# A two-layer diffusion backbone on one core: sums of squares in pieces with a product's step between, and roots spread by transposes

## The chip, the cores and the metric

The kernel runs on one core of a Trainium2 chip. The metric is the device time of one execution in microseconds; for a kernel it is the median of several runs. A profile is one execution taken by the hardware profiler. TensorE (PE, and PEld for its weight loads), VectorE (DVE), ScalarE (ACT), GpSimd (POOL) and SyncE (SP, which issues the transfers) run side by side and wait for each other through semaphores.

## The reference, cut to what matters

512 latent tokens and 256 context tokens of width 1024 pass two layers. Each layer norms its input with a modulation, projects it, runs three groups of heads (neighbourhood attention, differential attention, gated linear attention) on the projections, projects their outputs back onto the residual stream, norms again and runs a gated MLP with a convolution of width 3. Queries and keys of the first two groups are normed by head:

```python
def rms_norm(x, g):
    xf = x.astype(F32)
    y = xf * lax.rsqrt(jnp.mean(xf * xf, axis=-1, keepdims=True) + EPS)
    return (y * g.astype(F32)).astype(x.dtype)

xn = rms_norm(h, norm1[l]) * (1.0 + sc1) + sh1
qa = rms_norm(_heads(pl['qa'], NA_HEADS, HEAD_DIM), lp['qn_a'])
qb = rope_2d(rms_norm(_diff_heads(pl['qb']), lp['qn_b']), row, col)
o_b = rms_norm(o_b, lp['subln_b']) * (1.0 - lam_init)
```

The first line below the function is the modulated norm of the residual stream; the context tokens have their own. In the second layer the context tokens give keys, values and states only, and no outputs.

## The kernel before, in words

Activations lie with features on the partitions and tokens along the free axis, 128 features to a tile. Each fp32 product of the projections, the output projection and the MLP is made of three matmuls on rounded parts: high by high, high by low, low by high (`gemm_steps`, L251 to L253). A weight block of 512 KB is loaded (SP's queue), rounded by ScalarE (L262), and its remainder is taken by VectorE (L263), two blocks ahead.

In the mixer the order of TensorE's instructions is written out by hand. `weave` (L1121) takes a generator for the projections' products (`stream`, L606: the blocks named in `JOBS`, one after another; a step is three matmuls of 512 columns or six of 256, about every twelfth step is one of the modulation's own products, `ada_part`), and generators for the threads of the heads. The string `ORDER[layer]` says who comes next: a number is so many steps of the stream, a letter one step of a thread, lower case for the first two heads of a group and capitals for the second two. `next(stream, None)` does nothing once the stream is at its end. The letters that matter here:

- d: `da_prep` (differential attention: norms, rotation, stacks), a and b its two heads, e `da_out` (norms of its outputs);
- n: `na_prep` (neighbourhood attention: norms), l and r its two heads (for each tile of 128 queries: scores L897 to L899, softmax on VectorE and ScalarE, transposes in `to_tokens` L721, values L826);
- g: `gla_prep` (gated linear attention: gates L942 and L943, logarithms and running sums on ScalarE and VectorE), s its states, w its scores within chunks by levels (`gla_within`: L1018 to L1024 make a level's decays, two of the levels on POOL; L1049 is the product of the first two levels, L1061 that of the later ones), p and q its heads;
- h, f and o: the residual stream's return, the heads' outputs as operands, and the first part of the output projection, whose steps are products too.

`head_rms` (L673) is what the change touches in the threads d, e and n. It squares one or two tiles on ScalarE (L679), yields, and then sums the squares over a head's features: for each tile of 128 tokens one matmul whose weights are the 128 x 128 squares and whose moving operand is an indicator of 2 or 4 columns (L688). In layer 0 a call has 12 such products (d and n: 6 for the keys, 6 for the queries) or 6 (e); in layer 1, where queries have no context tokens, 10 or 4. An fp32 product is two records in the trace. The reciprocal roots come from `newton` (ten small operations of VectorE, L218 to L231) and are spread to the features by `head_bcast` (L706).

The modulated norm between the residual phases has its own sums (L489) and `newton`, and `norm_bcast` spreads the root of each token to all partitions by a matmul whose weights are the column of roots, broadcast, with the identity as moving operand (L494: two tiles of 128 tokens a call; `next_norm` calls it three times behind the output projection and three times behind the MLP in layer 0, and twice behind the output projection in layer 1). The very first norm does the same for six tiles in `begin` (L391).

PSUM tiles: `pg` (two buffers) for the stream's products, `pm` (two) for small ones, `pz` (two, of double size) for scores and broadcasts.

Of the kernel before, what the change touches and what calls it, by code (L numbers as in the profile page):

```python
# [27 lines left out]
EPS = 1e-6  # L28
NEG = -1e30
GW = 64  # L30
LEVELS = (64, 32, 16, 8, 4, 2, 1)
# row blocks of the output projection: those of the heads that are done first, and the last ones
OUT_A, OUT_B = (0, 1, 2, 3, 4, 5), (6, 7)
# dot products of the modulation's columns: along with a pair of blocks of the MLP, along with a block of its second product
CUTS = 2
ADA_F, ADA_D = 4, 2
# the order of the projections
JOBS = ("gates vb ka0 va0 qb1 kb1 kc0 vc0 qc0 qa1 ka1 va1 kc1 vc1 qc1 gc0 gc1 gc2 gc3",
        "qb0 kb0 vb qa0 ka0 va0 qb1 kb1 qa1 ka1 va1 gates kc0 vc0 qc0 gc0 gc1 kc1 vc1 qc1 gc2 gc3")
# the order of the first steps: norm, modulation by columns (scale, shift), rows of the products  # L40
# [13 lines left out]
# blocks of 32 columns whose windows of four say which copies a part of a stack goes to: (queries, keys) x (high, low)  # L54
# [3 lines left out]
# columns of the packed per-layer vectors  # L58
# [7 lines left out]
# column blocks of w_in (128 columns each)  # L66
# [4 lines left out]
class Lay:  # L71
    """Per-layer vectors on chip."""


class Rows:
    """Row blocks of a product's weights on two tiles of four."""
# [7 lines left out]
class Net:  # L84
# [53 lines left out]
    def setup(self, up):  # L138
        """Constants, and the first layer's vectors."""
# [14 lines left out]
    def tokens(self, p, up):  # L154
        """Two row blocks of the tokens."""
        x = up.tile([128, 2, TT], F32, name=f"x{p}")
        self.nc.sync.dma_start(out=x[:, :, :TL], in_=self.A["xT"][:, 2 * p:2 * p + 2])
        self.nc.sync.dma_start(out=x[:, :, TL:], in_=self.A["ctxT"][:, 2 * p:2 * p + 2])
        self.xs[2 * p], self.xs[2 * p + 1] = x[:, 0], x[:, 1]

    def silu_cond(self, up):
        """Twice silu of both conditioning vectors; the selector halves."""
# [28 lines left out]
    def layer_consts(self, y, up):  # L191
# [17 lines left out]
        # halved convolution weights (column 3 * f + j) and biases  # L209
# [4 lines left out]
    def newton(self, src, n, d):  # L214
        """rsqrt(src / d + EPS) of a compact [128, n]."""
# [8 lines left out]
        # a step of third order (to 8 / 3 of the root), and one of second order  # L224
# [21 lines left out]
    def gemm_steps(self, ps, w, ah, al):  # L246
        """A product; yields after every few steps of it."""
# [18 lines left out]
    def ada_part(self, y, part, pool, bufs):  # L266
        """A sixth of the modulation, 256 columns on each column tile; yields after every block of rows."""
# [22 lines left out]
    def ada_cols(self, fp, parts):  # L290
        """Sixths of the modulation [(layer, part)], columns on the partitions, by dot products of half columns; yields after each."""
# [24 lines left out]
    def ada_chunk(self, y, part, j, up):  # L316
        """256 columns of a sixth of the modulation: the blocks of rows on four column tiles."""
# [20 lines left out]
    def begin(self, y, up):  # L338
        """The first three products run on the scaled tokens; their outputs take the norm, and the shift's own product."""
# [42 lines left out]
        def norm():  # L382
# [5 lines left out]
            for (_, sl, _, _), p in zip(segs, (self.pg(TL), self.pm(TC))):  # L388
                t0 = sl.start // 128
                for t in range(t0, sl.stop // 128):  # L390
                    T.matmul(p[:, (t - t0) * 128:(t - t0 + 1) * 128], lhsT=r[:, t:t + 1].to_broadcast([128, 128]), rhs=self.ident,  # L391
                             start=True, stop=True)
                S.copy(bc[:, sl], p)
# [83 lines left out]
    def seg(self, g):  # L477
        """Stream, first token, operands of a segment."""
# [5 lines left out]
    def norm_bcast(self, accs):  # L484
        """PSUM [128, 256]: the reciprocal root mean square of each token on every partition."""
# [7 lines left out]
        for t in range(2):  # L493
            self.T.matmul(bc[:, t * 128:(t + 1) * 128], lhsT=r[:, t:t + 1].to_broadcast([128, 128]),  # L494
                          rhs=self.ident, start=True, stop=True)
        return bc

    def make_xn(self, y, xs, g, which, bc=None):
        """xs(k): the stream's tile and one for its norm (the same without bc: the tile is normed already)."""
# [30 lines left out]
    def pj(self, y, at, name, block, lat=True, ctx=True, perm=False, scale=1.0):  # L530
        """A block's product, on its way to DRAM, from where the head groups fetch it."""
# [17 lines left out]
    def cuts(self, y, name):  # L549
        """A weight that takes the place of two is made ready in parts."""  # L550
# [4 lines left out]
    def pjg(self, y, at, hd, ctxo):  # L555
        """A head's gate: twice its silu."""
# [14 lines left out]
    def pjv(self, y, at, name, block):  # L571
        """Values of 256 columns, tokens on the partitions."""
# [21 lines left out]
    def gates(self, y):  # L594
        """Low-rank gate activations: the weights' two parts side by side (the next product adds their sums)."""
# [35 lines left out]
    def finish(self, y, at, ctxo):  # L631
        """The heads' outputs as operands of the output projection."""
# [19 lines left out]
    def fetch(self, y, ea, hp, hd, cd):  # L652
        """The residual stream takes the place of the tiles that the heads needed first."""
# [10 lines left out]
    def out_first(self, y, ctxo):  # L664
        """The output projection of the heads that are done first."""
# [7 lines left out]
    def head_rms(self, at, xs, G, d, by=None):  # L673
        """Per (tile, token tile, group): reciprocal root mean squares (of the tile times by), compact. Yields ahead of the product."""
# [9 lines left out]
        for sq, (x, T) in zip(sqs, xs):  # L684
            offs.append(i)
            rhs = self.ones if G == 1 else self.ind[G]
            for t in range(T // 128):
                self.T.matmul(st[:, i * G:(i + 1) * G], lhsT=sq[:, t * 128:(t + 1) * 128], rhs=rhs, start=True, stop=True)  # L688
# [26 lines left out]
    def to_tokens(self, out, x, n):  # L715
        """x [128 features, n * 128 tokens] to out [128 tokens, n, 128 features]."""
# [15 lines left out]
    def da_prep(self, y, at, d, pr, ctxq):  # L732
# [8 lines left out]
        # the queries' norms go into the exponentials' scales  # L741
        qn = at.tile([128, TT], F32, tag="xn", name="xn", bufs=self.nxn)[:, :Tq]
        S.activation(qn, xq[:, :Tq], AF.Copy, scale=y.g[:, 1:2])
        for i, Tn in ((0, Tq), (1, TT)):
# [14 lines left out]
            # per component of 32 rows: high | low | high | low against high | low | low | high  # L759
# [22 lines left out]
        # reciprocals of the first softmaxes' sums  # L782
        d.rs = at.tile([128, 6, 2], F32, tag="rs", name="rs", bufs=2)

    def da_head(self, y, at, d, hh, ctxq):
        V, S, T = self.V, self.S, self.T
        for qt in range((TT if ctxq else TL) // 128):
# [18 lines left out]
            # times the first sum, whose reciprocal the outputs' norms take  # L806
# [13 lines left out]
    def values(self, d, qt, vs, ws):  # L820
        """Both heads' weights times values."""
# [7 lines left out]
    def da_out(self, y, at, d, pr, ctxq):  # L829
        """Norms of the outputs, and of the first softmaxes."""  # L830
# [34 lines left out]
    def na_head(self, y, at, d, pr, hh, ctxq):  # L865
# [3 lines left out]
        for qt in range(Tq // 128):  # L869
# [6 lines left out]
            # the scores' columns: segments (first, count, first key), and those with a bias  # L876
# [49 lines left out]
    def gla_prep(self, y, at, d, pr, ctxo):  # L926
        """Gates: 16 * log decay, then its running sums within chunks of 128, forward and backward."""
# [28 lines left out]
        # decays over whole chunks  # L956
# [5 lines left out]
    def gla_states(self, y, at, d):  # L962
        """States at the chunks' starts, both directions (context chunks are 4 and 5)."""
# [33 lines left out]
    def gla_within(self, y, at, d, ctxo):  # L997
        """Within chunks: pairs of halves at every level (whole blocks down to 32, then blocks of 32 side by side),
        then the diagonal (both directions: twice)."""
# [75 lines left out]
        # queries with the decay from their chunk's start, in the running sums' place  # L1075
# [5 lines left out]
    def gla_head(self, y, at, d, pr, hh, ctxo):  # L1081
        """Outputs, tokens on the partitions; root mean squares, then features on the partitions, and the gates."""
# [356 lines left out]
```

## Time and profile before

| | us |
|---|---|
| median of 3 runs | 1958.68 |
| lowest and highest run | 1957.72, 1968.63 |
| span of the profiled execution (first to last instruction) | 1956.1 |
| TensorE busy in it | 1874.8 |
| VectorE busy | 1234.8 |
| ScalarE busy | 774.1 |
| GpSimd busy | 107.1 |

Of the profiled execution the profile gives the span alone; it is 2.6 us below the median of the runs. The span holds two layers, one after the other: in layer 0 the mixer runs from about 60 to 560 us and the MLP to about 1130, in layer 1 the mixer from about 1160 to 1570 and the MLP to the end. In the rows, L12 is line 12 of the kernel; `pm<-k_ind,xn` reads "into tile pm from tiles k_ind and xn"; a bracket is the idle time ahead of an instruction and what ended it. PEclk is the clock granted to TensorE: 1.00 is 2.4 GHz, 0.50 is 1.2 GHz. A row of a stretch gives its bounds, its length, the busy time of PE, PEld, DVE, ACT and POOL (with the count of instructions; an engine without any is left out), then PEclk, the transfers' share and GB/s.

### The profile page before, as it was taken

To read this page: it belongs to the slowest core of one execution; us is meant where nothing else is said; L and a number is where in the kernel's file an instruction comes from. 1 tells how busy PE (TensorE), PEld (TensorE's weight loads), DVE (VectorE), ACT (ScalarE), POOL (GpSimd) and SP (SyncE) were. 2 spreads that over 40 slices of the span, in tenths; PEclk is the share of its full clock that TensorE was granted. 3 is DMA by queue.
4 is the path that set the end of the run, shared out by engine and by line. 5 is a ranking of instruction groups with operands and counts; after the bars stand their busy time and mean duration, and the time that the engine had idled before them with its cause. 6 is when DMAs were issued, how large, how long until landed. Compare 5 with 4: busy or idle time off the path is not lost. (4 is left out here: it accounts for less than half of the span.)

```text
span 1956.1 us, 33522 instructions
## 1 busy us (share of the span) xinstructions
PE 1874.8 (96%) x13598; PEld 1567.2 (80%) x13598; DVE 1234.8 (63%) x2554; ACT 774.1 (40%) x1350; POOL 107.1 (5%) x134
## 2 busy tenths in 40 slices
PE   8999999896999999999999999999996999999999
PEld 6778878774788888888888987878885788888887
DVE  6437575767669786588577563656576675445353
ACT  4536565455234331232133343645545343223232
POOL 2100000101020000000000110000012020000000
PEclk9989999897999999999999999999998989999999
DMA  9423242326122444234434223222433223332322
GB/s 323 138 92 111 92 146 98 115 98 204 54 74 92 124 129 149 94 125 130 139 109 127 95 68 130 84 81 68 143 106 101 65 72 97 97 97 86 109 94 100
DMA packets 90874, 217.93 MB, mean 111 GB/s; under 512 B 10464, under 2 KB 21472, under 8 KB 90592
## 3 DMA queue, kind: packets, MB, share of 16 engines
q1 hardware_dynamic: 90720, 215.79, 33.8%
q8 instruction: 107, 1.75, 0.4%
q14 instruction: 47, 0.39, 0.1%
HBM read 190.06 MB, written 25.69 MB: 110 GB/s over the span
## 5 line engine op out<-in xcount | busy, mean ns | idle before, releaser
L262 ACT CAST wh<-wr 128x1024 fp32r<-128x1024 f32 (+3 forms) x205 | 200.0, 978 | 415.9 <-PE pg L252 222.2
L263 DVE TENSOR_TENSOR wl<-wr,wh 128x1024 fp32r<-128x1024 f32 (+3 forms) x205 | 232.3, 1137 | 168.4 <-ACT wh L262 166.3
L252 PE MATMUL pz<-axl,wh 128*128 128x512 f32 (+1 forms) x752 | 288.3, 383 | 2.6 <-DVE axl L511 2.5
L251 PE MATMUL pz<-axh,wh 128*128 128x512 f32 (+1 forms) x752 | 287.8, 383 | 0.8 <-ACT axh L510 0.7
L253 PE MATMUL pz<-axh,wl 128*128 128x512 f32 (+1 forms) x752 | 287.0, 382 | 0.0
L252 PEld LDWEIGHTS pz<-axl,wh 128*128 128x128 f32 x752 | 142.3, 189 | 29.6 <-DVE axl L511 4.5
L251 PEld LDWEIGHTS pz<-axh,wh 128*128 128x128 f32 x752 | 142.3, 189 | 27.6 <-ACT axh L510 1.8
L253 PEld LDWEIGHTS pz<-axh,wl 128*128 128x128 f32 x752 | 142.3, 189 | 26.9
L308 DVE SCALAR_TENSOR_TENSOR wj<-wc,cb 128x512 bf16<-128x512 f32 x224 | 154.4, 689 | 6.2 <-DMA wc<-in_w_ada_t_dram 1.0
L251 PE MATMUL pg<-axh,wh 128*128 128x512 f32 x344 | 152.9, 445 | 2.7 <-ACT axh L262 2.5
L252 PE MATMUL pg<-axl,wh 128*128 128x512 f32 x344 | 139.3, 405 | 1.8 <-DVE axl L263 1.8
L253 PE MATMUL pg<-axh,wl 128*128 128x512 f32 x344 | 139.0, 404 | 0.0
L251 PE MATMUL pg<-gh,wh 128*128 128x512 f32 (+1 forms) x352 | 133.3, 380 | 0.0
L253 PE MATMUL pg<-gh,wl 128*128 128x512 f32 (+1 forms) x352 | 132.6, 377 | 0.0
L252 PE MATMUL pg<-gl,wh 128*128 128x512 f32 (+1 forms) x352 | 132.0, 375 | 0.0
L1161 DVE SCALAR_TENSOR_TENSOR h<-pg,ada,h 128x512 f32<-128x512 f32 (+1 forms) x80 | 53.5, 669 | 95.0 <-PE pg L253 94.8
L252 PE MATMUL pm<-acl,wh 128*128 128x256 f32 x352 | 99.8, 283 | 0.0
L253 PE MATMUL pm<-ach,wl 128*128 128x256 f32 x352 | 99.6, 283 | 0.0
L251 PE MATMUL pm<-ach,wh 128*128 128x256 f32 x352 | 99.5, 283 | 0.0
L801 DVE TENSOR_REDUCE sm<-pz 128x1 f32<-128x768 f32 (+1 forms) x80 | 67.4, 847 | 45.2 <-PE pz L800 44.5
L251 PEld LDWEIGHTS pg<-axh,wh 128*128 128x128 f32 x344 | 67.2, 195 | 30.8 <-issue 15.7
L1240 ACT ACTIVATE th<-cv 128x512 f32<-128x512 f32 x66 | 37.0, 561 | 121.2 <-DVE cv L1237 121.2
(387 smaller groups left out, 4194.9 us busy)
## 6 DMA issues: line engine op xcount, KB each, us to landing
wc<-in_w_ada_t_dram SPq DMA_DIRECT2D x112, 256.0 KB, 2.9
wr<-in_w_in_dram SPq DMA_DIRECT2D x45, 512.0 KB, 3.8
wr<-in_w_g_dram SPq DMA_DIRECT2D x44, 512.0 KB, 3.5
wr<-in_w_u_dram SPq DMA_DIRECT2D x44, 512.0 KB, 3.4
wr<-in_w_d_dram SPq DMA_DIRECT2D x31, 448.0 KB, 3.2
ar<-in_w_ada_dram SPq DMA_DIRECT2D x48, 256.0 KB, 3.3
ar<-in_w_ada_dram SPq DMA_DIRECT2D x16, 512.0 KB, 7.5
wr<-in_w_d_dram SPq DMA_DIRECT2D x16, 512.0 KB, 3.5
```

The source lines that it names most:

```text
L251: self.T.matmul(ps, lhsT=wh[:, k, :], rhs=ah[k], start=(k == 0), stop=False)
L252: self.T.matmul(ps, lhsT=wh[:, k, :], rhs=al[k], start=False, stop=False)
L253: self.T.matmul(ps, lhsT=wl[:, k, :], rhs=ah[k], start=False, stop=(k == n - 1))
L262: self.S.copy(hi, x)
L263: (eng or self.V).tensor_tensor(out=lo, in0=x, in1=hi.bitcast(F32), op=ALU.subtract)
L308: V.scalar_tensor_tensor(out=junk, in0=w, scalar=0.5, in1=cb[:, i, h * 512:h * 512 + 512], op0=ALU.mult, op1=ALU.mult, accum_out=acc[:, k, ...
L801: V.tensor_reduce(out=sm[:, c:c + 1], in_=s, op=ALU.max, axis=AX.X, negate=True)
L1161: self.late = V.scalar_tensor_tensor(out=h, in0=ps, scalar=y.ada[part][:, o, s:s + 1], in1=h, op0=ALU.mult, op1=ALU.add).ins
L1240: S.activation(th, c, AF.Tanh)
```

## The change

`head_rms` yields the mark `FILL` ahead of the third, fifth, seventh ... product of a call; `weave` answers each mark with one step of the projections' stream and then continues the same thread, before it reads on in the order string. The strings are unchanged. In `norm_bcast` and in the first norm the spreading matmuls become transposes of the broadcast column of roots (the same operands, one record instead of two). Comments and docstrings, which the diff also takes out, are left out here.

```diff
+FILL = "fill"
...
 def head_rms(self, at, xs, G, d, by=None):
...
             for t in range(T // 128):
+                if i and i % 2 == 0:
+                    yield FILL
                 self.T.matmul(st[:, i * G:(i + 1) * G], lhsT=sq[:, t * 128:(t + 1) * 128], rhs=rhs, start=True, stop=True)
                 i += 1
...
 def weave(self, stream, threads, order):
...
                 for _ in range(int(n or 0)):
                     next(stream, None)
-                if c:
-                    next(threads[c], None)
+                while c and next(threads[c], None) is FILL:
+                    next(stream, None)
...
 def norm(): (in begin)
-                    T.matmul(p[:, (t - t0) * 128:(t - t0 + 1) * 128], lhsT=r[:, t:t + 1].to_broadcast([128, 128]), rhs=self.ident,
-                             start=True, stop=True)
+                    T.transpose(p[:, (t - t0) * 128:(t - t0 + 1) * 128], r[:, t:t + 1].to_broadcast([128, 128]), self.ident)
...
 def norm_bcast(self, accs):
-            self.T.matmul(bc[:, t * 128:(t + 1) * 128], lhsT=r[:, t:t + 1].to_broadcast([128, 128]),
-                          rhs=self.ident, start=True, stop=True)
+            self.T.transpose(bc[:, t * 128:(t + 1) * 128], r[:, t:t + 1].to_broadcast([128, 128]), self.ident)
```

The ends of the two order strings, where the stream's last steps stand (the stream has 284 steps in layer 0 and 256 in layer 1; the numbers of a string add up to one more):

```
layer 0: ...wpqLR2RpqppRqqGLG2L1R1GSR1RL1L4p9R2RL1RqWL3R2RLR1fRWRffffffhhooSWSoSoSoWSWSooo...
layer 1: ...ws1s3w1w1wpq5ppqq4p2G1GqGSW15fffffffoWSooSWSoSooWooSoSWooo...
```

## Rows read from the trace of the kernel before

**Rows 1.** The page: TensorE's clock in 40 slices, and one group of transfers

```profile
PEclk9989999897999999999999999999998989999999
...
wr<-in_w_in_dram SPq DMA_DIRECT2D x45, 512.0 KB, 3.8
```

**Rows 2.** The sums of squares, line 688: all records of the run

```profile
L688 PE MATMUL pm<-k_ind,xn x216: 165/251/354, 87.7 to 1395.5; 128*128 128x2 f32 x64, 128*128 128x4 f32 x44
```

**Rows 3.** Timeline of TensorE, 118 to 141 us: start, duration, line, product, count

```profile
118.86 0.39 PE L253 MATMUL pg<-axh,wl 128*128 128x512 f32 x1
...
119.09 2.73 PE L688 MATMUL pm<-k_ind,xn 128*128 128x2 f32 x24
...
130.75 1.22 PE L770 MATMUL pm<-hl,stk 32*128 32x512 f32 x2
...
131.90 2.83 PE L706 MATMUL pz<-k_ident,ny 128*64 128x128 f32 x24
...
139.63 0.73 PE L770 MATMUL pm<-hl,stk 32*128 32x512 f32 x2
...
140.29 0.50 PE L251 MATMUL pg<-axh,wh 128*128 128x512 f32 x1
...
140.62 0.39 PE L252 MATMUL pg<-axl,wh 128*128 128x512 f32 x1
```

**Rows 4.** Stretches behind calls of the sums: length, engines' busy time, PEclk, DMA

```profile
91.70:95.10 3.40, 3.40 (x13) 1.36 (x12) 2.49 (x9) 1.16 (x2) 0.00 (x0) 0.50 0.32 91
...
122.40:139.40 17.00, 17.00 (x79) 10.87 (x78) 5.90 (x16) 1.79 (x3) 0.00 (x0) 0.50 0.21 69
...
177.10:180.40 3.30, 3.30 (x11) 2.16 (x10) 2.72 (x12) 0.86 (x2) 0.00 (x0) 0.50 0.15 40
...
263.00:266.40 3.40, 3.40 (x26) 3.23 (x27) 2.59 (x14) 2.53 (x4) 0.00 (x0) 1.00 0.00 0
...
358.00:364.70 6.70, 6.70 (x29) 5.61 (x33) 4.31 (x18) 1.34 (x4) 0.00 (x0) 0.50 0.01 4
...
378.50:385.20 6.70, 6.70 (x32) 6.17 (x32) 4.25 (x11) 2.74 (x3) 0.00 (x0) 0.50 0.08 22
...
1194.30:1197.60 3.30, 3.30 (x9) 2.20 (x8) 2.67 (x11) 0.62 (x1) 0.01 (x1) 0.50 0.69 231
...
1272.80:1279.50 6.70, 6.70 (x21) 5.50 (x22) 2.90 (x11) 0.95 (x3) 1.28 (x1) 0.50 0.45 137
```

**Rows 5.** Timeline of TensorE: four transposes, and four records of spreading products

```profile
427.48 0.66 PE L721 MATMUL pm<-k_ident,np 128*128 128x128 f32 x4
...
427.89 0.47 PE L251 MATMUL pg<-axh,wh 128*128 128x512 f32 x1
...
587.85 0.68 PE L494 MATMUL pm<-k_ident,ny 128*128 128x128 f32 x4 [0.85 <-DVE ny L231]
...
588.29 0.36 PE L253 MATMUL pz<-axh,wl 128*128 128x256 f32 x1
```

**Rows 6.** End of layer 0's stream: all engines, the stream's tiles alone, timeline

```profile
430.30:468.30 38.00, 29.73 (x208) 21.62 (x207) 30.08 (x63) 21.26 (x37) 4.79 (x4) 0.90 0.35 120
...
430.30:468.30 38.00, 19.65 (x117) 13.57 (x117) 4.03 (x10) 1.95 (x4) 0.90 0.35 120
...
459.16 1.76 DVE L1024 TENSOR_TENSOR lv<-lv,qk 128x1536 f32<-128x1536 f32 x1 [3.01 <-ACT lv L1023]
...
461.30 1.94 PE L276 MATMUL pg<-ar,csil 128*32 128x256 f32 x16 [4.60 <-DVE x L566]
...
468.27 1.99 PE L1049 MATMUL pz<-lv 64*64 64x64 f32 x64
```

**Rows 7.** End of layer 1's stream: the stream's tiles alone, timeline of TensorE

```profile
1481.00:1490.90 9.90, 9.82 (x42) 7.81 (x42) 0.66 (x1) 0.60 (x1) 1.00 0.18 65
...
1502.28 1.13 PE L1049 MATMUL pz<-lv 64*64 64x64 f32 x32 [11.38 <-DVE lv L1024]
...
1506.75 1.13 PE L1049 MATMUL pz<-lv 64*64 64x64 f32 x32 [3.34 <-DVE lv L1024]
```

More of the change, by code (lines that the diff above doesn't have):

```diff
@@ L71 @@
 class Lay:
+    pass
 class Rows:
```

## The prediction

> **What bounds the kernel now.** I read the page first, then the rows of the line that the change splits, then the stretches behind it, then the two places where the order of TensorE's work runs dry. The page shows TensorE busy for 1874.8 of 1956.1 us (the table above), and a granted clock below full in several slices [rows 1]. So TensorE's own order is the path nearly everywhere, and time is won by a higher clock or lost by a wait on it. The time to start from is this one profile's span, 1956.1 us; the median of the runs shown, 1958.68 us, is 2.6 us above it, and I add changes to the median.
>
> The sums of squares are 216 records, two for each of 108 products (12 calls of the helper) [rows 2]. A call of 24 records at 119.09 us takes 2.73 us, 0.11 us a record, with two columns each: the array has almost nothing to stream [rows 3]. What follows is the point. Behind seven of the twelve calls the clock goes to 0.50, the 1.2 GHz level. One step of the differential attention's stacks took 1.15 us there (130.75 to 131.90), and 0.66 us at the 2.4 GHz level (139.63 to 140.29): 43% of a slow stretch is lost [rows 3]. The slow stretches behind the calls last 3.4, 17.0, 3.3, 6.7, 6.7, 3.3 and 6.7 us, and each begins during its call or a few us behind it; behind the other five the clock stays at 1.00, as from 263.0 us behind a call of 12 records [rows 4].
>
> **The change part by part.**
>
> *Where the steps go.* A FILL comes ahead of the third, fifth, ... product of a call, and each one takes one step of the projections' stream. In layer 0 calls have 12, 12 and 6 products, so 5 + 5 + 2 FILLs for a pair of heads and 24 for the layer; in layer 1 they have 10, 10 and 4, so 4 + 4 + 1, and 18. The order strings are not changed. Counting their numbers, the stream (284 steps in layer 0, 256 in layer 1) ended with one call to spare; now it ends 24 and 18 steps sooner, and the numbers near the end of the strings find nothing. No work is added: steps move from the end of the mixer to the middle.
>
> *The clock, a gain.* Between two pieces of four records (4 x 0.11 = 0.44 us) there are now three products of 512 columns, about 0.7 us (118.86 to 119.09 is one: 0.23 us) [rows 3]. TensorE then streams for more than half of the time, where it did for hardly any. I take the six stretches in which a call of 20 or 24 records alone precedes the fall as gone: 3.4 + 17.0 + 3.3 + 6.7 + 3.3 + 6.7 = 40.4 us; at 43% that is 17.4 us [rows 3, 4]. The one at 378.5 us lies behind a call of only 12 records that follows other small products; I count half of 6.7 x 0.43 = 2.9, so 1.5. Gain 18.9 us; the bounds are 0 (the pieces don't hold the clock) and 20.3 us (all seven go).
>
> *The seams, a loss.* A large product that follows small ones starts late: its successor comes 0.33 us after it (140.29 to 140.62) rather than 0.23 [rows 3]. 42 more seams at 0.09 us cost 3.8 us. Below it is 0, if the next weights are loaded ahead; above it is twice as much, 7.6 us, at the low clock. I take 3.8, the value at the clock that I expect.
>
> *The transposes, a small gain.* The spreading product is two records and the trace's transposes are one. Four spreading records take 587.85 to 588.29, 0.44 us, and four transposes 427.48 to 427.89, 0.41 us for twice as many tiles [rows 5]. So each of the eight calls for a modulated norm (three in each of two places of layer 0, two in layer 1) gets about 0.22 us shorter, 1.8 us, and the first norm's six tiles save 0.6. Where TensorE waits for the norm this is on the path, and where it does not it is TensorE's time; 2.0 us, between 0 and 2.6.
> Here the Trainium skill speaks against the change: "TensorE: Matmul & The Clock Gate", Part 4 (PE-mode transpose), says that a transpose does not count as TensorE being busy as a matmul does, so that the full clock does not engage for it. By that rule the eight calls would come nearer to a fall of the clock; that is the last rival. The transposes of the trace stand among larger products [rows 5], so no row here settles it.
>
> *Dry end of layer 0, a loss.* The second gate product of the second pair of heads ends at 430.3 us, and the first scores within chunks of this pair (L1049) start at 468.27. In these 38.0 us the tiles of the stream hold TensorE for 19.65 us, the last of them at the low clock; all but one of the 24 missing steps fell here, and at the full clock they are 19.65 - 0.43 x 1.94 (the modulation's products at 461.30) = 18.8 us [rows 6]. This work now stands ahead of that stretch, where TensorE is full, and delays its start by 18.8. In return the stretch can shrink, but not below its own chain: gates, logarithm, running sums, decays of two levels on VectorE, ScalarE and POOL. This had its last product of decays at 459.16 + 1.76 = 460.9 us, 30.6 us after the gates, with VectorE busy for 30.08 of the 38.0, of which 4.03 us belonged to the stream's tiles and leave too [rows 6]. Between 27 (the chain less those) and 38 us (nothing shrinks) I take 29, nearest to the chain that the trace shows. Loss 18.8 - 9 = 9.8 us, bounds 7.8 and 18.8. The wait of 4.60 us of the modulation's product for VectorE at 461.30 goes [rows 6], but what is late next is this chain.
>
> *Dry end of layer 1, a loss.* Here TensorE already waits: the stream ends at 1490.9 and L1049 follows at 1502.28 after 11.38 idle us, its second half at 1506.75 after 3.34 more [rows 7]. Fourteen steps, 9.82 us, lie between the gates and that wait, and 4 more ahead of the gates: 18 steps of 3 x 0.23 us, 12.4 us, are done sooner and push everything behind [rows 3, 7]. Of the 4 ahead of the gates (2.8 us) I let half come back, 1.4, an estimate: the transposes between the two gate products then wait for VectorE. VectorE's running sums are freed of two operations of 0.66 us on the stream's last tiles, 1.3 us [rows 7]. Loss 12.4 - 1.4 - 1.3 = 9.7 us; bounds 8.3 (all 2.8 and the 1.3 come back) and 12.4.
>
> *What else the moved steps issue.* Their weights' loads (SP's queue; 3.8 us for a block that feeds 8 or 12 steps [rows 1]), ScalarE's rounding, VectorE's remainder and the copy out move with them. Each step's work keeps its order in each queue, and the blocks are about 8 us of TensorE apart, so I count nothing; if a FILL met a block not yet ready, sums and the square root behind them would wait for it. The sums' PSUM tile is held for about 3.5 us longer, while no other thread's product can come between. Nothing else is queued behind it on TensorE.
>
> Sum: -17.4 - 1.5 - 2.0 + 3.8 + 9.8 + 9.7 = +2.4 us. Forecast: no change that can be measured, 1958.7 + 2.4 = 1961.1 us; its own range is 1953 to 1969.
>
> **The rivals.**
>
> 1. *The dry ends shrink with the work.* If threads ran ahead as the stream does, the 19.5 us would be nothing: 1941.6 us. For it: 8.3 of the 38 us were idle on TensorE in layer 0, and its order, not the chain, held L1049 for the last 7 us. Against it: VectorE alone has 26 us of other work there, and in layer 1 it is TensorE that waits [rows 6, 7].
> 2. *The dry ends are paid in full (the other side).* Without steps between, the neighbourhood attention's rounds (scores, softmax, transposes, values) stand bare, at the low clock, and L1049 stays 38 us behind the gates. Then 18.8 + 12.4 = 31.2 instead of 19.5: 1972.8 us. The other terms make -17.1, so the kernel is slower from the point where the two stretches give back less than 14.1 of the 31.2; I count 11.7, and here it is 0. For it: 11.38 us of waiting at 1502.28 already; against it: the 4.60 us wait that goes.
> 3. *The clock falls all the same,* since each piece is still four small products and the steps between are single ones: the 18.9 us stay lost, 1980.0 us. For it: the slow stretch at 378.5 us, behind a call of only 12 records; against it: the steps at 139.63 us mix small and large products as thinly at the high clock [rows 3].
> 4. *Transposes let the clock fall at the norms.* Four more stretches of 3.4 us at 43% are 5.8 us: 1966.9 us. No row prices a transpose so, and eight short calls are little; its chance is small.
>
> **How the numbers follow.** Forecast 0.43, rival 1 0.15, rival 2 0.22, rival 3 0.10, rival 4 0.06, none of these 0.04. Within 1% is 1939.1 to 1978.3 us, about what a measurement of this kernel can tell from no change: forecast, rivals 2 and 4 and most of rival 1 lie inside. Faster by more needs rival 1 with the upper clock gain and no seams: 0.07. Slower by more is half of rival 3 and the upper ends of rival 2 and of the unnamed: 0.10. Same 0.83. The range leaves out rival 3 and about half of rival 1: 1942 to 1974 us.
>
> **What would show it.** Right: groups of four records of L688's line with three products of the stream between them; the clock at 1.00 behind the calls of 20 and 24; the stream's last product ahead of or near the second pair's gates in both layers; TensorE idle for about 20 us between the gates and L1049 in layer 1 (14.7 before); one record for each spread root. Wrong: the clock at 0.50 within 4 us of the split calls (rival 3), L1049 less than 24 or more than 34 us behind the gates in layer 0 (rivals 1, 2), new slow stretches at the norms (rival 4).

## The result, and the profile after

The changed kernel takes 1986.88 us (median of 4 runs, 1984.97 to 1987.51) against 1958.2 of before (the three runs of the table and one more, of 1951.24): a ratio of 1.0154, 95% interval 1.0113 to 1.0195. Here and below the ratio is an estimate from all runs and is not quite the quotient of the medians. The forecast of no change (1961.1 us) was wrong, and the time lies above its range. The profiled execution has a span of 1984.4 us, 28.4 more than that of before.

The page of the changed kernel: the span, the busy time of the engines, and the granted clock in 40 slices.

```profile
span 1984.4 us, 33478 instructions
...
PE 1870.5 (94%) x13576; PEld 1561.9 (79%) x13576; DVE 1233.7 (62%) x2554; ACT 775.9 (39%) x1350; POOL 110.7 (6%) x134
...
PEclk9999999985899999999999999999997989999999
```

TensorE is busy for 4.3 us less than before, and the kernel is 28 us longer: what was added is waiting. And the low clock has moved: the dips in slices 3 and 8 of [rows 1] are gone, and those in slices 10 (446 to 496 us) and 31 (1488 to 1538 us), where the two orders run out of steps, are deeper, with 5 instead of 7 and 7 instead of 8.

One split call, in the timeline of TensorE (start, duration, line, product, count):

```profile
121.38 0.50 PE L690 MATMUL pm<-k_ind,xn 128*128 128x2 f32 x4
121.74 0.48 PE L253 MATMUL pg<-axh,wh 128*128 128x512 f32 x1
122.05 0.40 PE L254 MATMUL pg<-axl,wh 128*128 128x512 f32 x1
122.29 0.40 PE L255 MATMUL pg<-axh,wl 128*128 128x512 f32 x1
122.52 0.50 PE L690 MATMUL pm<-k_ind,xn 128*128 128x2 f32 x4
122.88 0.48 PE L253 MATMUL pg<-axh,wh 128*128 128x512 f32 x1
```

The change does what it says (L690 is L688 of before). A piece of four records lets the next product start 0.36 us after it (121.38 to 121.74), 0.09 us a record instead of 0.11; the step behind it takes 0.78 us (121.74 to 122.52) instead of 3 x 0.23. The seam costs the 0.09 us that was forecast, and the piece gives as much back.

The stretches behind the calls, as [rows 4] (length, busy time of PE, PEld, DVE, ACT and POOL, PEclk, DMA), and the two ends:

```profile
127.00:144.00 17.00, 17.00 (x120) 11.94 (x119) 10.90 (x23) 6.63 (x11) 0.00 (x0) 1.00 0.24 86
...
366.00:372.80 6.80, 6.80 (x73) 5.16 (x76) 4.79 (x18) 1.88 (x4) 0.00 (x0) 1.00 0.39 130
...
1296.40:1303.20 6.80, 6.80 (x46) 6.06 (x45) 4.13 (x14) 2.63 (x5) 1.29 (x1) 1.00 0.43 128
436.80:484.60 47.80, 30.62 (x211) 20.87 (x208) 31.11 (x66) 23.23 (x40) 4.94 (x5) 0.50 0.20 69
1508.60:1539.30 30.70, 10.13 (x86) 7.07 (x87) 19.45 (x32) 14.89 (x17) 7.64 (x4) 0.50 0.09 31
```

Behind the calls the clock is now at 1.00, in those 17 us too that were at 0.50 before. At the end of layer 0's stream it is at 0.50 for 47.8 us on end, with TensorE idle for 17.2 of them.

To see where the 28 us came from I cut each mixer at two marks: G1, the first gate product of the second pair of heads (L942, in the changed kernel L944), and N, the norm's sums behind the mixer (L489, L490). Before: first call to G1, G1 to N, for layer 0 and then layer 1 (which I count from the norm's sums behind layer 0's MLP):

```profile
87.70:423.00 335.30, 326.73 (x2984) 260.47 (x2982) 202.50 (x470) 168.02 (x341) 12.30 (x19) 0.94 0.34 113
423.00:564.30 141.30, 120.69 (x1353) 95.26 (x1352) 97.20 (x199) 59.53 (x102) 13.79 (x16) 0.93 0.35 112
...
1131.10:1477.50 346.40, 334.58 (x2791) 276.67 (x2791) 212.54 (x493) 170.71 (x331) 16.94 (x28) 0.98 0.29 97
1477.50:1574.30 96.80, 77.74 (x819) 61.20 (x818) 68.25 (x129) 43.55 (x66) 17.16 (x14) 0.91 0.30 91
```

The same four in the changed kernel:

```profile
88.00:430.00 342.00, 330.41 (x3090) 264.63 (x3088) 207.63 (x481) 173.62 (x350) 13.24 (x19) 0.99 0.35 118
430.00:582.50 152.50, 117.82 (x1248) 91.65 (x1247) 91.89 (x188) 55.37 (x92) 13.78 (x16) 0.79 0.26 89
...
1147.40:1502.60 355.20, 339.21 (x2827) 280.02 (x2827) 212.79 (x487) 175.15 (x337) 20.35 (x28) 1.00 0.30 100
1502.60:1602.40 99.80, 70.18 (x777) 54.53 (x775) 67.68 (x133) 40.07 (x60) 16.20 (x14) 0.85 0.22 72
```

In layer 0, 106 records of TensorE have gone from behind G1 to ahead of it: 42 of 512 columns, 48 of 256 and 16 of the modulation, some 16 us at the full clock (0.23 and 0.12 us between successive starts; the modulation's counted at 0.04). The stretch up to G1 is only 6.7 us longer, and G1 comes 7.0 us later: the higher clock made TensorE's busy time some 12 us less than the old one and the 16 (330.4 for 326.7 + 16), but its waits are 3.0 us longer (11.6 for 8.6, length less busy time), so about 9 came back. But the stretch behind G1, relieved of that work, has become 11.2 us longer, at a clock of 0.79 instead of 0.93. In layer 1, 42 records (9.7 us) went the same way; G1 is 8.8 us later against the layer's start, although the busy time is some 5 us less than the sum, since the waits are 4.2 us longer (16.0 for 11.8); the stretch behind it is 3.0 us longer. With -1.9 between N of layer 0 and layer 1's start (566.8 us before, 564.9 after) the sum is 7.0 + 11.2 - 1.9 + 8.8 + 3.0 = 28.1 of the 28.4 us. These are differences of two single profiles; the experiments show how far such parts scatter.

The end of layer 0's stream in the timeline, as [rows 6] (a bracket is the idle time ahead and what ended it):

```profile
435.06 0.62 PE L278 MATMUL pg<-ar,csil 128*32 128x256 f32 x4 [1.67 <-DVE nt L231]
436.64 0.97 PE L278 MATMUL pg<-ar,csil 128*32 128x256 f32 x4 [0.95 <-DMA ar<-in_w_ada_dram]
...
442.03 1.06 PE L945 MATMUL pz<-asb,wa 64*128 64x256 f32 x2
...
459.42 1.09 PE L723 MATMUL pm<-k_ident,np 128*128 128x128 f32 x4 [8.34 <-DVE np L912]
...
473.47 1.12 PE L828 MATMUL pm<-wn,vn 128*64 128x128 f32 x6 [2.32 <-ACT wn L724]
...
478.49 0.66 PE L723 MATMUL pm<-k_ident,np 128*128 128x128 f32 x2 [1.79 <-DVE np L912]
479.08 2.84 PE L1051 MATMUL pz<-lv 64*64 64x64 f32 x96
```

The second gate product ends at 443.1 us and L1051 starts at 479.08: 36.0 us, where the forecast took 29 and before had 38.0. So the 11.2 us come from the two sides of this stretch: from G1 to the end of the second gate product 13.1 us instead of 7.3 (the waits for the modulation in the first two rows, and the low clock), and from L1051 to N 103.4 instead of 96.0.

The chain behind the gates did not get shorter: its last product of decays is the last of the next rows, and ends 31.4 us after the gates (30.6 before). The first row is of before, the others are of the changed kernel; L949 and L951 begin VectorE's part of the chain.

```profile
435.97 1.76 DVE L949 TENSOR_TENSOR lt<-B,lt 128x1536 f32<-128x1536 f32 x1 [0.59 <-ACT lt L948]
...
447.13 1.58 ACT L950 ACTIVATE lt<-lt,ones 128x1536 f32<-128x1536 f32 x1
...
451.11 0.48 DVE L1117 SCALAR_TENSOR_TENSOR xn<-pm,gq,xn 128x256 f32<-128x256 f32 x1 [0.78 <-PE pm L1115]
451.51 1.75 DVE L951 TENSOR_TENSOR lt<-B,lt 128x1536 f32<-128x1536 f32 x1
...
472.73 1.76 DVE L1026 TENSOR_TENSOR lv<-lv,qk 128x1536 f32<-128x1536 f32 x1 [3.01 <-ACT lv L1025]
```

In the 36 us VectorE is busy for 23.4, so it is not its load that sets this chain. From L951 to the last of VectorE's decays (L1024, done at 463.07) it takes 11.6 us instead of 14.6, so the work that left did free it. But in before L949 starts as soon as the logarithm of ScalarE is done; here the logarithm is done at 448.71 and L951 starts 2.8 us later, behind operations of VectorE's queue that wait for TensorE's products at the low clock (L1117). Another 1.1 us go at the two hand-overs to ScalarE and POOL behind it. And TensorE, left with the neighbourhood attention's small products, waits for each softmax in turn (8.34, 2.32 and 1.79 us of the rows); the last such round stands between the end of the chain at 474.5 us and L1051.

The end of layer 1's stream, as [rows 7]:

```profile
1508.51 1.05 PE L1115 MATMUL pm<-k_ident,ox 128*128 128x128 f32 x4 [4.31 <-DVE ox L1106]
...
1511.36 1.06 PE L945 MATMUL pz<-asb,wa 64*128 64x256 f32 x2
1530.83 1.14 PE L1051 MATMUL pz<-lv 64*64 64x64 f32 x32 [18.41 <-DVE lv L1026]
1534.12 1.14 PE L1051 MATMUL pz<-lv 64*64 64x64 f32 x32 [2.16 <-DVE lv L1026]
```

Here TensorE idles for 20.6 us ahead of L1051, as forecast (about 20; 14.7 before), and 4.31 more ahead of the second gate product.

### The profile page after: what moved, and what is told of

It is laid out like the page before. It is cut to its first block, busy times and chain, and to the rows that moved or that the text cites. A ratio compares the mean times of both kernels' runs of the same rounds, so it can differ in the third digit from the quotient of the medians.

```text
span 1984.4 us, 33478 instructions
## 1 busy us (share of the span) xinstructions
PE 1870.5 (94%) x13576; PEld 1561.9 (79%) x13576; DVE 1233.7 (62%) x2554; ACT 775.9 (39%) x1350; POOL 110.7 (6%) x134
## 5 line engine op out<-in xcount | busy, mean ns | idle before, releaser
L807 ACT ACTIVATE P<-pz,sm,ny 128x768 f32<-128x768 f32 (+1 forms) x80 | 72.6, 908 | 32.3 <-DVE sm L806 29.3
```

Of the source, the lines that this page charges most:

```text
L807: S.activation(P[:, c, :nk], s, AF.Exp, bias=sm[:, c:c + 1], scale=rq, accum_out=sm[:, 2 + c:3 + c])
```

## The experiments

The ratios are against runs of the kernel before on the same chip, with 95% intervals. The theory held at first was that moving the steps out of the ends costs the time and the clock behind the calls is a gain; the rivals are in the expectations.

**The steps paid back from the next numbers.** Each mark's step is taken off the numbers that follow, none below 1, so that the streams end where they did.

```diff
+        owed = 0
...
-                for _ in range(int(n or 0)):
+                n = int(n or 0)
+                back = min(owed, max(n - 1, 0))
+                owed -= back
+                for _ in range(n - back):
                     next(stream, None)
                 while c and next(threads[c], None) is FILL:
+                    owed += 1
                     next(stream, None)
```

> The kernel after, but each step of the stream that a mark takes is paid back from the next numbers of the order string (never below one step a number), so the stream reaches its end at the same letter as before the change. Theory A (the clock gain is real and the dry ends ate it): both dry ends are as before, no slow stretch behind the split calls, 1958 - 14 to 19 = 1939 to 1944 us. Rival B (splitting the sums costs more than the clock gives: seams, later roots): at or above 1958 us.

1978.51 us, ratio 1.0103 (1.0071 to 1.0136): the expected gain is missing. The ends are as before in layer 0 (141.3 us from G1 to N; 100.7 in layer 1, where four profiles with the order of before have 96.8 to 101.6). But where steps were taken, TensorE waits, and the clock falls behind it, as in this place of layer 1 (a wait for the operands of the differential attention's stacks, then the stretch behind it):

```profile
1198.81 0.50 PE L772 MATMUL pm<-hl,stk 32*128 32x512 f32 x1 [1.90 <-ACT hl L264]
...
1199.70:1213.40 13.70, 13.70 (x69) 7.75 (x70) 1.78 (x3) 1.70 (x3) 0.00 (x0) 0.50 0.22 71
```

Layer 0 comes out as in before (N at 563.1 us), layer 1 20.8 us longer up to N. About half of that is TensorE's waiting, 41.0 us instead of 30.9, and half the clock, at 0.50 for 54.6 us instead of 30.7. The way of paying back cost what the ends had saved.

**The calls whole, the steps behind each.**

```diff
+                marks = 0
                 while c and next(threads[c], None) is FILL:
+                    marks += 1
+                for _ in range(marks):
                     next(stream, None)
```

> The kernel after with the calls whole again: all the steps that a call's marks take run behind its last product. The dry ends stay as in the kernel after, the splitting goes. Theory A: the slow stretches behind the calls come back in part, about 14 us more than the kernel after, 1995 to 2003 us. Rival B (the splitting is the cost): back to about 1960 us.

1989.86 us, 1.0174 (1.013 to 1.0217): neither. Against the changed kernel the difference is some 3 us and the intervals overlap, so that the cut itself is not shown to be worth anything. Up to G1 of layer 0 the two profiles say why:

```profile
87.40:428.40 341.00, 334.68 (x3089) 267.73 (x3087) 208.49 (x481) 173.51 (x350) 13.24 (x19) 0.97 0.35 118
```

The changed kernel took 342.0 us for the same records. Its cuts kept the clock higher (at 0.50 for 6.8 us, here for 17.0), but it waited for 11.6 us and this kernel for 6.3. The changed kernel's longest wait there, for the roots of a cut call that ends later, does not occur here; its row in the changed kernel:

```profile
278.86 2.00 PE L708 MATMUL pz<-k_ident,ny 128*64 128x128 f32 x24 [4.14 <-DVE ny L699]
```

So the pieces do hold the clock, which here still falls behind six of the twelve calls of the two layers, for 3.4 or 6.8 us each, and behind none in the changed kernel. But steps right behind a whole call already shorten the slow stretches (3.4 us from 125.4, where before had 17), and what cutting adds to the clock it takes back in waits. The loss at the ends is nearly the same (148.5 and 100.5 us from G1 to N).

**The transposes alone,** in the kernel before (the two edits at L391 and L494).

> The kernel before with the transposes alone. Theory A: 1 to 3 us less than before, 1955 to 1957 us, and no new slow stretch at the norms. Rival D (transposes let the clock fall at the norms): up to 6 us more, 1964 us.

1954.4 us, 0.9992 (0.9968 to 1.0015): no difference that can be measured. Its windows: first call to G1, G1 to N, and the norms behind layer 0's mixer and MLP.

```profile
86.90:416.60 329.70, 322.02 (x2983) 256.25 (x2981) 202.34 (x470) 167.77 (x341) 12.30 (x19) 0.96 0.34 115
416.60:557.10 140.50, 120.76 (x1354) 95.27 (x1353) 97.11 (x199) 59.43 (x102) 13.81 (x16) 0.93 0.34 113
...
557.10:590.00 32.90, 29.95 (x227) 27.58 (x227) 28.99 (x85) 16.08 (x36) 9.24 (x12) 1.00 0.10 33
1122.00:1152.00 30.00, 27.95 (x191) 24.46 (x192) 24.08 (x76) 12.99 (x27) 3.20 (x4) 1.00 0.18 63
```

The clock is at 1.00 over both norms, and the time leaves no room for the last rival's 6 us (the upper end of the interval is 3). Behind layer 1's mixer, where the other two calls are, the clock is at 0.50 for 10.2 us with transposes as in before. That is also the answer of this case to the Trainium skill's "TensorE: Matmul & The Clock Gate", Part 4 (PE-mode transpose), by which the full clock does not engage for a transpose: eight calls of two, among other products, did no harm that can be measured.

The first row says something else. Up to G1 this is the order of before, and it took 329.7 us instead of 335.3, with the clock at 0.50 for 27.3 us instead of 37.5. One profile of an unchanged order differs from another by 6 us there, so the 9 us that came back in layer 0 against the profile of before are under 4 against this one. A third profile of this order, of the kernel below with cuts in layer 1 alone, sides with it:

```profile
87.60:416.80 329.20, 321.94 (x2983) 256.11 (x2981) 202.07 (x470) 167.71 (x341) 12.29 (x19) 0.96 0.34 115
```

**The clock kept up at the ends.** Where a number finds the stream ended, a product that nobody reads is computed. It adds work and takes away no wait.

```diff
+    def idle_product(self):
+        self.T.matmul(self.pg(384), lhsT=self.ident, rhs=self.cosT[:, :384], start=True, stop=True)
...
-                    next(stream, None)
+                    if next(stream, self) is self:
+                        self.idle_product()
```

> The kernel after, and wherever a number of the string finds the stream at its end, a product of 384 columns of constants that nobody reads (0.64 us at the high clock; 44 of them, so 28 us of useless work). Theory C (the dry ends are long because the clock is low there): layer 0's end becomes as short as before, about 11 us less, layer 1's stays: 1974 to 1980 us. Rival E (the ends are a chain of waits through the softmaxes and decays, and the clock matters little): 0 to 10 us more, 1987 to 1997 us.

1982.19 us, 1.0137 (1.0097 to 1.0177), between the two expectations. It is 4.7 us below the changed kernel, but the intervals overlap, so that a gain is not shown; what is shown is that the 28 us of added products did not make it longer. Its windows from G1 to N, and two lines of TensorE's timeline:

```profile
430.90:577.60 146.70, 125.34 (x1297) 93.65 (x1296) 91.57 (x188) 55.44 (x92) 13.09 (x16) 0.90 0.28 93
1504.10:1599.40 95.30, 78.50 (x807) 59.65 (x806) 64.18 (x126) 39.16 (x58) 17.12 (x14) 0.91 0.23 73
```

```profile
454.65 5.97 PE L1124 MATMUL pg<-k_cosT,k_ident 128*128 128x384 f32 x18
...
479.14 2.84 PE L1051 MATMUL pz<-lv 64*64 64x64 f32 x96
```

With the clock at 0.90 the stretch of layer 0 is 146.7 us: of the 11.2 that it had grown by, 5.8 go. Eighteen records of the idle products fill the place of the 8.34 us wait, and L1051 starts at 479.1 as without them. But the second gate product ends at 445.4 here, 2.3 us later, as the idle products stand ahead of it too: from there the chain of decays takes 29.4 us instead of 31.4 (L951 is now 0.8 us behind the logarithm, not 2.8) and L1051 comes after 33.8 us instead of 36.0. Behind L1051 another 4.9 us go. What is left, 5.4 us, is open: the clock is still below that of before (0.93), and the added products hold TensorE themselves.

**The same steps sooner, without cuts.** The kernel before, with 24 and 18 steps more ahead of the first call, which the ends lack as in the change.

```diff
-     "35d1d1d7d1d1
+     "59d1d1d7d1d1
...
-     "45d1d1d5d1d1
+     "63d1d1d5d1d1
```

> The kernel before (no marks, no transposes) with the first number of each order string raised by the steps that the marks take, 35 to 59 and 45 to 63: the stream is 24 and 18 steps ahead from the start and ends so much sooner. Nothing else changes, so it prices the two dry ends alone. Theory A (the dry ends are the loss): 1955 + 28 in layer 0 + 10 to 12 in layer 1 = 1990 to 1995 us. Rival F (ending sooner costs what I forecast, 10 and 10): 1975 us. Rival B (the marks are the loss): 1955 to 1960 us.

2016.51 us, 1.0293 (1.0244 to 1.0342): a loss is there without any cut, and larger than any of the three expected. Layer 0, from 88.0 us, where the changed kernel has its first call (this one at 105.0, behind the added steps), to G1, and G1 to N:

```profile
88.00:451.20 363.20, 351.49 (x3090) 280.67 (x3088) 208.63 (x481) 172.95 (x350) 13.49 (x19) 0.92 0.33 111
451.20:598.70 147.50, 112.25 (x1248) 87.49 (x1247) 91.89 (x188) 55.42 (x92) 13.78 (x16) 0.81 0.28 92
```

Behind G1 the stretch again gives nothing back, but it is no longer than the changed kernel's 152.5 (and 99.5 us in layer 1): what is larger lies ahead of G1. The first row holds the same 3090 records as the changed kernel's, and takes 363.2 us at a clock of 0.92, not 342.0 at 0.99: the clock was at 0.50 for 54.5 us, not for 6.8. Most of that is not the work of the cuts, since the kernel with whole calls and the steps right behind them had 17.0 us at 0.50 and took 341.0 us for this stretch: it is the place of the steps, next to the calls or far ahead of them. So this kernel does not price the ends alone, as it was meant to.

**The steps taken from the numbers just ahead of each call,** both layers; calls cut, ends as before. An example, the start of layer 0's string:

```diff
-     "35d1d1d7d1d1d1d1d1d2d1d1d3d5n1nd
+     "30d1d1d7d1d1d1d1d1d2d1d1d2d1n1nd
```

> The kernel after with the marks' steps taken out of the numbers just ahead of each call (never below one step a number; three that don't fit are taken out of later numbers), so the stream is at the old place behind every call and both dry ends are as before. Theory A (the marks' clock gain is real if the steps come from where they are spare): 1940 to 1948 us. Rival G (a step taken from anywhere near leaves that place bare, as in the run that paid back behind the calls): 1955 to 1980 us.

1961.42 us, 1.004 (1.002 to 1.0061). Undoing the dry ends recovers 1.1% of the 1.5, but there is no gain against before: layer 0 is 3.6 us shorter up to N than in the profile of before (and some 3 longer than in the two others with its order, 557.1 and 557.8), layer 1 10.7 longer. First call to G1 in layer 0, and in layer 1 its start to G1:

```profile
84.10:418.60 334.50, 321.14 (x3008) 258.65 (x3006) 205.92 (x472) 170.22 (x344) 11.94 (x19) 0.97 0.34 114
...
1126.90:1479.80 352.90, 333.82 (x2785) 275.34 (x2785) 213.99 (x493) 170.99 (x331) 17.80 (x28) 0.99 0.29 96
```

Again the cuts are paid for in waits: TensorE idles for 13.4 us in the first stretch (8.6 in before, 7.7 with the transposes alone) and 19.1 in the second (11.8). Nor does a cut call always hold the clock: at the call of 12 records of the differential attention's outputs it fell here at 371.6 us for 10.2 us, behind a wait of 1.89 us within the call, and it fell at that call in two of the kernels below as well, as it did behind it in before (378.5 us).

**The modulation's steps sooner,** every tenth instead of every twelfth step of the changed kernel, so that none is left between the gates:

```diff
-i % 12 == 11
+i % 10 == 9
```

> The kernel after with a step of the modulation's products behind every 10th step of the stream instead of every 12th, so none of them is left for the stream's end. Theory H (the modulation's last steps, which wait for their weights between the two gate products, lengthen layer 0's end): the second gate product follows the first about 5 us sooner and the kernel gains 3 to 6 us, 1981 to 1984 us. Rival E (the end is bound by the chain behind the gates whatever stands between them): 1987 us, no change.

1987.12 us, 1.017 (1.0137 to 1.0202): no gain. The second gate product follows the first after 5.3 us instead of 10.2, and the stretch from G1 to N is 143.1 us, but the first is now at 436.7 instead of 430.0, and N at 579.9 us. So those steps and their waits (1.67 and 0.95 us above) lengthen that stretch, and cost as much in another place.

**One layer at a time.** Three kernels with cuts in one layer alone and the transposes kept:

```diff
-                if i and i % 2 == 0:
+                if self.fills and i and i % 2 == 0:
...
+        self.fills = y.l == 0
```

The first has layer 0 cut with its steps taken ahead of each call (layer 0's string as in the kernel of that name above, so that the end keeps its steps), the second has layer 0 cut as in the change, the third layer 1 (`y.l == 1`).

> Calls split in layer 0 alone, with the steps for them taken out of the numbers just ahead of each call, so that its stream ends where it ended in before; layer 1 as in before; transposes kept. If the parts add up (theory A): layer 0's first norm sums at 560.7 us as in e6 (564.3 in before), some 1 to 2 us less at the norms behind, layer 1 from 1131 on as before (443 us to its norm sums): 3 to 6 us under before, 1948 to 1951, ratio 0.997 to 0.9985, the first kernel of the case that is not slower. Rival: layer 0's gain was a coincidence of one profile, or is handed back in the MLP: a ratio of 1.000 or above.

> The change in layer 0 alone (its 24 steps, orders untouched), layer 1 as before; transposes kept. If the trace of after was read rightly: the norm sums of layer 0 at about 582 us (564.3 in before), G1 to them 152.5; layer 1 from its start to its norm sums 443 as before; span +16 (18.2 less 1.9 at the norms), ratio 1.008. Rival: the layers' losses are tied through what overlaps (weights of layer 1, DMAs), and one layer alone gives under 10 or over 22.

> The change in layer 1 alone (its 18 steps), layer 0 as before; transposes kept. If the trace of after was read rightly: layer 0's norm sums at 564, the MLP's end near 1129, layer 1 to its norm sums 455 (443 in before), so span +10 (11.8 less 1.9), ratio 1.005. Rival: under 4 (the loss came from layer 0's delay of loads), or over 16.

The first: 1953.85 us, 1.0001 (0.9985 to 1.0017). The second: 1975.53, 1.0114 (1.0079 to 1.0149). The third: 1970.96, 1.0077 (1.005 to 1.0104). Their windows from G1 to N, of layer 0 in the first, then of layer 0 in the second:

```profile
420.10:561.30 141.20, 121.21 (x1353) 95.95 (x1352) 97.52 (x199) 59.63 (x102) 13.80 (x16) 0.93 0.34 112
```

```profile
430.20:580.30 150.10, 114.00 (x1247) 88.82 (x1246) 91.44 (x188) 55.28 (x92) 13.80 (x16) 0.81 0.27 90
```

The third, layer 1:

```profile
1478.40:1577.90 99.50, 69.91 (x777) 54.38 (x776) 67.64 (x133) 40.01 (x60) 16.20 (x14) 0.85 0.22 72
```

The first two have the same cuts in the same layer and differ only in which steps fill them: those from just ahead, or those from the end. That is 1.1%, some 22 us, for layer 0 (16 was expected). Layer 1 costs some 15 us by its ratio (10 was expected). The profile of the third shows only 3.7 us more span than that of before, and its other runs were 8 to 12 us above the profiled one: one profile is no measure here, the ratio is. The two layers add up to 1.9%, within the interval of the whole change, so the losses of the two layers need no tie between them. And with the ends left alone, cuts give no gain that can be measured in layer 0: the hope for 3 to 6 us fell with the second case of its expectation. No version measured here beats the kernel before.

## Why the prediction was wrong

It was rival 2 (the ends paid in full), and more than in full: 1972.8 us were given for it.

- *The dry end of layer 0* is the step that failed. It let a stretch of 38 us give 9 of the 18.8 moved back, since VectorE would be freed of 4.03 us, and took 29 us for what is left. What came instead: 36.0 us from the gates to L1051, outside the bound named for it (34), and 35 to 37 in the four other kernels without idle products that lack those steps. VectorE's own part of the chain did shrink, by 3.0 us, but the chain lost that again where its operations stand in a queue behind others that wait for TensorE at the low clock (2.8 us ahead of L951, and 1.1 later). And the forecast looked at the stretch up to L1051 alone, and held the 103.4 us behind it (96.0 before) at no change. The whole stretch from G1 to N was 140.5 to 142.1 us in the six kernels with those steps in it, and 143.1 to 152.5 in the six without: the steps stood in waits and cost nothing there. Ahead of G1 they cost 16 us by the estimate above. And taking them out made the clock fall for 47.8 us on end, which the forecast's sum did not hold; idle products that raised the clock took 5.8 us off, and the rest stays open. The term is 16 + 11.2 = 27 by the profiles, and some 22 by the two kernels that differ in it; not 9.8, nor within its bounds (7.8 to 18.8).
- *The dry end of layer 1*: 9.7 + 3.0 = 12.7 us against 9.7 (bounds 8.3 to 12.4). The mechanism was right, with the wait of 20 us where it was said to be, and the wait for the transposes between the gates too (4.31 us). The 3.0 are within the scatter of this stretch: 96.8 to 101.6 us in four profiles with the order of before, 99.5 to 101.9 in the five without the steps and without idle products. So it gave nothing back here either.
- *The clock behind the calls*: the mechanism was right for this kernel, since the clock was at 1.00 in all the stretches priced; rival 3 is out for it. Against the profile of before the size was right as well: TensorE's busy time is some 17 us less than the sum of the old and the moved work, 18.9 were forecast. But some 7 us of new waits took that down to 10, and against the profile of the transposes alone it is about 2. The forecast summed the slow stretches of one execution, and two others of the same order had 10 us fewer of them up to G1. And the cut itself bought nothing that can be measured, as whole calls with the steps behind them showed.
- *The seams*: 0, not 3.8. The 0.09 us are there, but a piece of four records is shorter by the same.
- *The transposes*: -1.9 us in the trace between N and layer 1's start, of which a slow stretch of 3.4 us that is gone at 566 us makes 1.5; nothing by the median. The forecast of 2.0 was of the right order, but by luck: such a stretch of 3.4 us comes at this norm with transposes too, in three of the kernels above.
- *What else the steps issue* was put at nothing, and that was wrong by the 7 us of waits: 3.0 in layer 0, where the wait of 4.14 us for the roots at 278.9 us is new (one of 1.24 us for the modulation near by is gone), and 4.2 in layer 1. The prediction had named the way, a call that is held longer, and gave it no price.

The chances were wrong in the same place: slower by over 1% had 0.10, and rival 2 was priced as if the end could at worst give nothing back. A stretch that waits on a chain can also get longer when work leaves it.

## What to carry to other kernels

A step that fills a wait is free where it stands, and here cost its time in each of the other places where it was put; before moving independent work, count what is left to fill the waits of the place that it leaves, from the last point where all orders agree to the next one, not to the first late instruction. A fuller middle at the full clock was bought with a bare end at half of it. And a gain that is summed over slow stretches of the clock in one profile should be compared with a second profile of the same kernel.

## What the runs showed that was not expected

- Products that nobody reads, 28 us of them where the stream was at its end, did not make the kernel longer (1982.19 us, 1986.88 without): the clock over that stretch of layer 0 rose from 0.79 to 0.90, and the work behind the chain took 98.5 us instead of 103.4.
- TensorE's low clock reached a chain that has no product in it: the first operation of VectorE's part started 2.8 us after its operand was there, behind others in the queue that waited for TensorE. It is 2.8 us in four kernels, and 0.8 with the idle products.
- The same order of TensorE up to G1 took 335.3 us in one profile and 329.7 and 329.2 in two others, with the clock at 0.50 for 37.5, 27.3 and 27.3 us.
- Cut into pieces of four, the small fp32 products of 2 columns take 0.09 us a record rather than 0.11.
- In the stretch from G1 to N of layer 0, 105 records fewer took nearly the same busy time of TensorE (117.8 against 120.7 us), as the clock was 0.79 instead of 0.93.
